# One transformer block on one core: x first in the queue, k/v weights in three pieces, identity products ahead of x

## The chip, the cores and the metric

The kernel runs on one core of one Trainium2 chip. The metric is the device time of one execution in microseconds. Of the kernel before, three runs are at hand: 1082.71, 1082.85 and 1082.98 us; the median is 1082.85.

## The reference

One encoder block, sequence 1024, width 1024, all in float32:

```
h = rmsnorm(x, norm1_g)
q, k, v, u = split(h @ w_in)              # widths 512, 128, 128, 512
a = attention(rope(rmsnorm(q)), rope(rmsnorm(k)), v)   # 8 query heads, 2 key/value heads of 64
p = (pool(u) - u) per group @ pool_w + pool_b, times pool_scale   # windows 2, 4, 8, 16
x = x + concat([a, p]) @ w_out
x = x + (silu(h2 @ w_gate) * (h2 @ w_up)) @ w_down     # h2 = rmsnorm(x, norm2_g), width 2816
```

## The kernel before

**Products.** Most operands of a product are split into two rounded parts, `hi` and `lo` (float32r), and a product is three TensorE passes over these parts (`PASSES`). Every split costs one copy (`hi`) and one subtraction (`lo`, line 355) on VectorE, ScalarE or GpSimd.

**The start.** x comes as eight tiles of 128 rows (`load_x`, line 434). TensorE turns each tile by eight transposes of 128x128 against the float32 identity (`turn_x`, line 474); ScalarE writes the `hi` part of each out of PSUM, scaled by a gain out of `pk` (line 464), and VectorE the `lo` part (line 466). `load_w` fetches weight blocks of `w_in` into one of three raw buffers (`NRAW`) and splits them into scratch tiles `wk`, of which there are 36 (`NSLOT`). The weights of k and v together are 256 columns wide and 8 blocks of 128 rows deep; before, they come as two pieces of four blocks, 512 KB each. `kv_tile(t)` (line 490) multiplies tile `t` of the turned x by them: per block k, three products of 256 columns.

**The order.** All is issued in the order written in the code. x's tiles are worked on in the groups [0], [1], [2, 3], [4, 5, 6, 7]. First the whole of group 0 is turned; then `weave` (line 933) alternates one k-step of k/v of a group with one transposed block of the next group. So the products of tile 0 are interleaved with the transposes of tile 1, and the transposes of tile 1 begin behind the first k-step of tile 0. TensorE carries this list out strictly in order. `stats_x` (line 447) adds the squares of a tile on ScalarE and takes the reciprocal root on VectorE by some twelve tiny operations (lines 362 to 373).

**The planner.** The order on VectorE, ScalarE and GpSimd, and which of them takes a split, come from `Flow`: it keeps a model of the time of each engine and of the DMA (`flow.load`), is run six times without a chip ahead of the build, and ranks jobs by the time at which TensorE needs them. In this model TensorE's steps cost double until 12 us (`COLD`). Both `load_x` and `load_w` tell it when data arrive.

**Queues.** All loads of the start go out on SyncE's queue in program order: `pk` (line 1523), x tile 0 in two halves, two weight pieces, x tiles 1 to 7, then the first u weights, gains, rope tables and the next u weights. A fetch into a raw buffer waits until the readers of that buffer's last content are done. `ident` is made by GpSimd at the very start, and `identr`, its rounded copy, by VectorE at line 384.

**PSUM.** `bank()` gives one of four banks of 512 columns, `bank2()` one of two double ones; `turn_x` uses both in turn.

Of the kernel before, what the change touches and what calls it, by code (L numbers as in the profile page):

```python
# [18 lines left out]
P = 128  # L19
# [3 lines left out]
NK = D // P  # L23
# [3 lines left out]
AW = NQ * HD  # L27
KW = NKV * HD
# [16 lines left out]
NRAW = 3  # L45
RIM, GAP = 120, 80
K = {
    "pieces": 2, "groups": [[0], [1], [2, 3], [4, 5, 6, 7]], "take": [0, 3], "tables": 2, "spread": [1],
    "ahead": [22, 39], "turn_k": 50, "wq": [60], "mix": [56, 62, 10, 30], "prep_q": [20], "turn_q": [37],
    "wo": [33, 39, 52, 62], "score": [40, 41, 42, 43, 47, 49, 52, 54, 57, 59, 61, 63, 63], "fold": 1,  # L50
    "out": [0, 0, 0, 2, 1, 2, 1, 2], "wo2": [3, 9, 10, 10, 16, 16], "mix_c": 5, "norm": 6, "next_prep": 8,
# [212 lines left out]
def act(n, extra=0.0):  # L264
    return "A", 0.1 + 0.00097 * n + extra


def dve(n):

    return "D", max(0.16, 0.07 + 0.00119 * n)  # L270
# [19 lines left out]
def block_kernel(  # L290
# [4 lines left out]
    nc = tc.nc  # L295
# [6 lines left out]
    w_in2, w_out2, w_gate2, w_up2, w_down2 = w_in[0], w_out[0], w_gate[0], w_up[0], w_down[0]  # L302
# [22 lines left out]
    flow = Flow(ranks)  # L325
    ffn = []

    def bank(dt=F32):
        flow.claim("b1", 4)
        return ps1.tile([P, 512], dt, tag="b1", name="b1")  # L330

    def bank2(dt=F32):
        flow.claim("b2", 2)
        return ps2.tile([P, 1024], dt, tag="b2", name="b2")

    def split(hi, lo, src, n, both=False):
        way = flow.quicker(act(n), dve_copy(n), pool_scale(n)) if both and not ffn else act(n)
        yield way
        if way[0] == "A":
            nc.scalar.activation(hi, src, AF.Copy)  # L340
        elif way[0] == "D":
            nc.vector.tensor_copy(hi, src)
        else:
            nc.gpsimd.tensor_scalar(hi, src, 1.0, 1.0, op0=ALU.mult, op1=ALU.mult)
        if both:
            yield from combine(n, lo, src, hi.bitcast(F32), ALU.subtract)
        else:
            yield dve(n)
            nc.vector.tensor_tensor(lo, src, hi.bitcast(F32), op=ALU.subtract)  # L349
# [33 lines left out]
    identr = held.tile([P, P], F32R, name="identr")  # L383
# [7 lines left out]
    def work(dt=F32, n=D):  # L391
        return wk.tile([P, n], dt, tag="wk", name="wk")
# [3 lines left out]
    def fetch(view, src, n=D):  # L396
        raw = rawp.tile([P, n], F32, tag="raw", name="raw")
        nc.sync.dma_start(view(raw), src)
        old = readers[-NRAW] if len(readers) >= NRAW else None
        readers.append(None)  # L400
        after = 0.0 if old is None else old.ready
        return raw, flow.load(P * n * 4, after), len(readers) - 1

    def consume(token, job):
        readers[token] = job
        return job
# [3 lines left out]
    def hT(a, k, c0, n):  # L410
        h, c = divmod(c0, HALF)
        o = (k % 2) * HALF + c
        return hs[a][h][k // 2][:, o:o + n]

    def load_w(col, n, per, apart=False):

        res = []
        for j in range(NK // per):
            raw, at, tok = fetch(
                lambda v: v.rearrange("p (k n) -> p k n", n=n),  # L420
                w_in2[j * per * P:(j + 1) * per * P, col:col + n].rearrange("(k p) n -> p k n", p=P))
            hi, lo = work(F32R), work(F32R)
            if not apart:
                job = consume(tok, flow.add(split(hi, lo, raw, D, both=True), at))
            for k in range(per):
                c = slice(k * n, (k + 1) * n)
                if apart:
                    job = consume(tok, flow.add(split(hi[:, c], lo[:, c], raw[:, c], n, both=True), at))
                res.append((hi[:, c], lo[:, c], job))
        return res  # L430
# [3 lines left out]
    def load_x(ts, pieces=1):  # L434
        n = D // pieces
        for t in ts:
            for i in range(pieces):
                nc.sync.dma_start(qp[:, t, i * n:(i + 1) * n], x2d[t * P:(t + 1) * P, i * n:(i + 1) * n])
                at = flow.load(P * n * 4)
                for k in range(i * n // P, (i + 1) * n // P):  # L440
                    x_at[t, k] = at
# [16 lines left out]
    def turn_x(ts):  # L458
        n = len(ts) * P
        c0 = ts[0] * P  # L460

        def evacuate(hi, lo, pt, k):
            yield act(n, 0.05)
            nc.scalar.activation(hi, pt[:, :n], AF.Copy, scale=g1[:, k:k + 1])
            yield dve(n)
            nc.vector.scalar_tensor_tensor(lo, pt[:, :n], g1[:, k:k + 1], hi.bitcast(F32), op0=ALU.mult, op1=ALU.subtract)

        for k in range(NK):
            flow.now = max([flow.now] + [x_at[t, k] for t in ts])
            wide = k % K["wide"] == K["wide"] - 1  # L470
            pt = bank2()[:, 0:512] if wide else bank()
            flow.tensor(0.107 * len(ts))
            for i, t in enumerate(ts):
                nc.tensor.transpose(pt[:, i * P:(i + 1) * P], qp[:, t, k * P:(k + 1) * P], ident)
            job = flow.add(evacuate(hT(0, k, c0, n), hT(1, k, c0, n), pt, k))
            flow.hold("b2" if wide else "b1", job)
            for t in ts:
                x_turned[t, k] = job
            yield

    E4 = HD // 4
    kv_job, kt_job, q_job = {}, {}, {}
# [410 lines left out]
    class OutProj:  # L893
# [5 lines left out]
        def run(self, n):  # L899

            for _ in range(min(n, NK - self.i)):
                k = KORDER[self.i]
                if self.i == 0:
                    self.py = bank()
                    if self.rows is None:
                        self.xr, at, self.tok = fetch(lambda v: v, x2d[self.t * P:(self.t + 1) * P, self.cs], 512)
                    else:
                        self.xr, self.tok = self.rows[0][:, self.cs], self.rows[2]
                j = attn_job[self.t]
                flow.tensor(0.681, wo[k][2], *(j[:1] if k >= 4 else j[1 + k // 2:2 + k // 2]))  # L910
                for i, (a, b) in enumerate(PASSES):
                    nc.tensor.matmul(self.py, mix[self.t][a][:, k, :], wo[k][b][:, self.cs], start=(self.i == 0 and i == 0), stop=(self.i == NK - 1 and i == 2))  # L912
                self.i += 1
                if self.i == NK:
                    job = flow.add(self.close())
                    flow.hold("b1", job)
                    x2_job[self.t, self.c] = consume(self.tok, flow.add(self.squares(job)))
# [15 lines left out]
    def weave(tiles, ts=None):  # L933
        turns = turn_x(ts) if ts else None
        for i, b in enumerate([b for g in [kv_tile(t) for t in tiles] for b in [g] * NK]):
            next(b, None)
            if turns and i % len(tiles) == 0:
                next(turns, None)
# [33 lines left out]
    def after(jobs):  # L972
        yield jobs
# [535 lines left out]
    def take_w(i):  # L1509
        g = order[i]  # L1510
        wus[g] = load_w(AW + 2 * KW + g * P, P, NK)

    def lean(phase):

        flow.load_of["D"] = K["load"][phase]
# [4 lines left out]
    ordered = tc.manual_schedule(engines=None)  # L1520
    ordered.__enter__()
    lean("x")
    nc.sync.dma_start(pk, packed)
    load_x([0], K["pieces"])
    wkv = load_w(AW, 2 * KW, 4, apart=True)
    load_x(range(1, NT))
    groups = K["groups"]
    run(turn_x(groups[0]))
    kf, tab_job = [], None
    for i, ts in enumerate(groups):  # L1530
# [17 lines left out]
    for i, g in enumerate(order):  # L1548
        for _ in pool_group(g):
            if at("spread", step):  # L1550
                spread_r(dgs, ones)
            for w in range(2):
                if K["ahead"][w] == step:
                    take_w(2 + w)
                if K["mix"][w] == step:
                    run(pool_mix(order[w]))
            if step == K["turn_k"]:
                flow.tensor(0, *kf)
                kt = k_turn()
            if step >= K["turn_k"]:  # L1560
                next(kt, None)
            if at("wq", step):
                wq = load_w(0, AW, 2)
            step += 1
# [148 lines left out]
```

## Time and profile before

| | us |
|---|---|
| median of three runs | 1082.85 |
| the profiled execution | 1083.04 |
| its span, first to last instruction | 1081.0 |
| TensorE busy (matmul) | 1061.1 |
| VectorE busy | 742.1 |
| ScalarE busy | 513.6 |
| GpSimd busy | 459.0 |

How to read it: PE is TensorE's matmul stream, PEld its weight loads, which run beside the matmuls; DVE is VectorE, ACT ScalarE, POOL GpSimd, SP SyncE. Times in a timeline count from the start of the span. A row of a timeline merges neighbours of one line; its second number runs from the start of the first to the modelled end of the last, so rows of TensorE overlap, and the pace of its steps is read from the starts. In brackets stands how long the engine was idle before, and what ended that. In the chain, each piece is the work that the next one waited for.

### The profile page before, as it was taken

How to read it: one execution, taken by the hardware profiler on the slowest of the kernel's cores; microseconds unless marked ns; L12 is line 12 of the kernel's file. 1: busy time of each engine (PE TensorE's matmuls, PEld its weight loads, DVE VectorE, ACT ScalarE, POOL GpSimd, SP SyncE). 2: the span in 40 equal slices, each digit the busy share in tenths (PEclk: the TensorE clock that was granted, in tenths of full speed). 3: DMA queues.
4: the chain of work that ended last, by engine and by line, in shares of the span. 5: the costliest groups of instructions: out<-in, count | busy, mean ns of one | idle time of the engine just before them, and what ended most of it. 6: DMA issues, size and time to landing. Idle time of an engine off the chain costs nothing.

```text
span 1081.0 us, 13923 instructions
## 1 busy us (share of the span) xinstructions
PE 1061.1 (98%) x5114; PEld 876.2 (81%) x5114; DVE 742.1 (69%) x1210; ACT 513.6 (48%) x912; POOL 459.0 (42%) x371
## 2 busy tenths in 40 slices
PE   7999999999999999999999999999999999999998
PEld 6887877878888888878878887888788878888787
DVE  7888678788776766784984479355954496448845
ACT  6614478666666654633343433434433443343340
POOL 3153444444223223463643555345534464445431
PEclk9999999999999999999999999999999999999999
DMA  7212110000000100221023102220212013110114
GB/s 260 69 40 79 39 59 30 10 21 10 20 21 11 30 21 30 59 98 39 19 68 109 39 1 78 78 79 1 78 59 76 23 33 104 59 40 20 40 58 156
DMA packets 42707, 58.47 MB, mean 54 GB/s; under 512 B 4240, under 2 KB 32784, under 8 KB 42640
## 3 DMA queue, kind: packets, MB, share of 16 engines
q1 hardware_dynamic: 42640, 57.59, 16.9%
q8 instruction: 40, 0.66, 0.2%
q14 instruction: 27, 0.22, 0.1%
HBM read 53.39 MB, written 4.19 MB: 53 GB/s over the span
## 4 chain that ended last, share of the span: by engine, by line
PE 79%; DVE 10%; issue 3%; POOL 3%; ACT 3%; DMA 1%; SPq 0%; POOLq 0%; ACTq 0%; DVEq 0%
PE b L1180 36%; PE b L912 8%; PE b L1498 8%; PE b L875 5%; PE b L832 5%; PE b L862 4%; PE b L688 4%; PE b L601 3%; DVE wk L355 3%; POOL wk L355 2%; PE b L1445 2%; DVE qp L1460 2%; PE b L490 2%; DVE ring L355 1%; DVE nm L841 1%
## 5 line engine op out<-in xcount | busy, mean ns | idle before, releaser
L1180 PE MATMUL b<-wk,ring 128*128 128x512 f32 x1872 | 426.8, 389 | 1.2 <-POOL ring L355 0.9
L1180 PEld LDWEIGHTS b<-wk,ring 128*128 128x128 f32 x1872 | 351.0, 188 | 75.6 <-POOL ring L355 1.8
L340 ACT ACTIVATE ring<-raw 128x512 fp32r<-128x512 f32 x130 | 81.5, 629 | 121.2 <-PE b L1180 59.9
L851 POOL TENSOR_SCALAR wk<-wk,rsm 128x1024 f32<-128x1024 f32 x64 | 75.0, 1180 | 132.9 <-PE b L862 40.7
L349 DVE TENSOR_TENSOR wk<-b,wk 128x512 fp32r<-128x512 f32 (+1 forms) x160 | 102.0, 659 | 42.5 <-ACT wk L340 42.1
L340 ACT ACTIVATE wk<-b 128x512 fp32r<-128x512 f32 (+1 forms) x160 | 90.4, 577 | 82.6 <-PE b L862 65.6
L355 POOL TENSOR_TENSOR ring<-raw,ring 128x512 fp32r<-128x512 f32 x49 | 63.3, 1292 | 149.5 <-ACT ring L340 136.0
L1498 PE MATMUL b<-raw,ring 128*128 128x512 f32 x480 | 113.4, 393 | 1.1 <-DVE qp L1460 1.1
L355 DVE TENSOR_TENSOR ring<-raw,ring 128x512 fp32r<-128x512 f32 x81 | 63.7, 789 | 72.2 <-ACT ring L340 71.7
L1498 PEld LDWEIGHTS b<-raw,ring 128*128 128x128 f32 x480 | 88.6, 188 | 24.3 <-DVE qp L1460 3.8
L1460 DVE TENSOR_TENSOR qp<-qp,b 128x512 f32<-128x512 f32 (+1 forms) x157 | 100.5, 673 | 9.0 <-PE b L1445 8.9
L912 PE MATMUL b<-wk 128*128 128x512 f32 x384 | 102.5, 397 | 0.0
L355 POOL TENSOR_TENSOR wk<-wk 128x512 fp32r<-128x512 f32 (+3 forms) x51 | 71.5, 1409 | 43.5 <-ACT wk L340 20.3
L832 PE MATMUL b<-kT,wk 128*128 128x512 f32 x256 | 89.4, 431 | 0.3 <-ACT wk L808 0.3
L875 PE MATMUL b<-wk,vv 128*128 128x512 f32 x256 | 82.7, 399 | 3.9 <-DVE wk L349 3.9
L841 DVE TENSOR_REDUCE nm<-b 128x1 f32<-128x1024 f32 x64 | 78.0, 1219 | 11.3 <-PE b L832 10.2
L1498 PE MATMUL b<-wk,ring 128*128 128x512 f32 x360 | 83.3, 389 | 0.0
L912 PEld LDWEIGHTS b<-wk 128*128 128x128 f32 x384 | 70.7, 188 | 14.9
L1498 PEld LDWEIGHTS b<-wk,ring 128*128 128x128 f32 x360 | 67.5, 188 | 14.2
L862 PEld LDWEIGHTS b<-ident,wk 128*128 128x128 f32 x512 | 63.6, 140 | 16.5
L862 PE MATMUL b<-ident,wk 128*128 128x128 f32 x512 | 76.4, 272 | 0.0
L843 ACT ACTIVATE wk<-b,nm 128x1024 f32<-128x1024 f32 x64 | 71.4, 1116 | 10.4 <-DVE nm L841 9.5
(144 smaller groups left out, 1445.1 us busy)
## 6 DMA issues: line engine op xcount, KB each, us to landing
raw<-in_w_gate_dram SPq DMA_DIRECT2D x22, 512.0 KB, 3.7
raw<-in_w_up_dram SPq DMA_DIRECT2D x22, 512.0 KB, 3.9
wk<-in_w_down_dram SPq DMA_DIRECT2D x20, 512.0 KB, 4.7
raw<-in_w_in_dram SPq DMA_DIRECT2D x10, 512.0 KB, 3.8
raw<-in_w_out_dram SPq DMA_DIRECT2D x8, 512.0 KB, 3.5
out_dram<-qp SPq DMA_DIRECT2D x15, 256.0 KB, 2.0
qp<-in_x_dram SPq DMA_DIRECT2D x7, 512.0 KB, 9.7
raw<-in_x_dram SPq DMA_DIRECT2D x14, 256.0 KB, 2.8
```

The source lines that it names most:

```text
L340: nc.scalar.activation(hi, src, AF.Copy)
L349: nc.vector.tensor_tensor(lo, src, hi.bitcast(F32), op=ALU.subtract)
L355: (nc.gpsimd if way[0] == "G" else nc.vector).tensor_tensor(dst, a, b, op=op)
L832: nc.tensor.matmul(s[:, c * 512:(c + 1) * 512], qT[t][0][:, h * P:(h + 1) * P], kT[:, kv, b, c * 512:(c + 1) * 512], start=(b == 0), stop= ...
L841: nc.vector.tensor_reduce(nm, s, axis=AX, op=ALU.max, negate=True)
L851: nc.gpsimd.tensor_scalar(pe, pe, rs, 1.0, op0=ALU.mult, op1=ALU.mult)
L862: nc.tensor.transpose(pt[:, j * P:(j + 1) * P], pe[:, c * P:(c + 1) * P], ident)
L875: nc.tensor.matmul(po[t, kv], vt, ps[:, b], start=(c == 0 and b == 0), stop=(c == NT - 1 and b == 1))
L912: nc.tensor.matmul(self.py, mix[self.t][a][:, k, :], wo[k][b][:, self.cs], start=(self.i == 0 and i == 0), stop=(self.i == NK - 1 and i == 2))
L1180: nc.tensor.matmul(bank_, w[0][:, a, i], x[:, b], start=(start and i == 0 and j == 0), stop=(stop and i == PARTS - 1 and j == 2), skip_gro ...
L1460: nc.vector.tensor_tensor(dst, dst, src, op=op)
L1498: nc.tensor.matmul(banks[t][0], x[:, a, t * P:(t + 1) * P], y[:, b], start=(own == name and i == 0 and j == 0), stop=(i == 1 and j == 2), ...
```

## The change

x tile 0 is loaded ahead of `pk`, in one piece of 512 KB. The weights of k and v come in three pieces of 2, 2 and 4 blocks (256, 256 and 512 KB), each in a raw buffer and a pair of scratch tiles of its own. Ahead of the first transpose, `keep_busy(24)` issues 24 TensorE products of the rounded identity with itself (128 columns each) into one PSUM bank that nobody reads. The existing `after([])` is an empty job that tells the planner that the bank is free. The planner's model isn't told of the 24 products.

```diff
@@ -45,7 +45,7 @@
 NRAW = 3
 RIM, GAP = 120, 80
 K = {
-    "pieces": 2, "groups": [[0], [1], [2, 3], [4, 5, 6, 7]], "take": [0, 3], "tables": 2, "spread": [1],
+    "busy": 24, "pieces": 1, "groups": [[0], [1], [2, 3], [4, 5, 6, 7]], "take": [0, 3], "tables": 2, "spread": [1],
     "ahead": [22, 39], "turn_k": 50, "wq": [60], "mix": [56, 62, 10, 30], "prep_q": [20], "turn_q": [37],
     "wo": [33, 39, 52, 62], "score": [40, 41, 42, 43, 47, 49, 52, 54, 57, 59, 61, 63, 63], "fold": 1,
     "out": [0, 0, 0, 2, 1, 2, 1, 2], "wo2": [3, 9, 10, 10, 16, 16], "mix_c": 5, "norm": 6, "next_prep": 8,
@@ -415,10 +415,12 @@
     def load_w(col, n, per, apart=False):
 
         res = []
-        for j in range(NK // per):
+        k0 = 0
+        for per in ([per] * (NK // per) if isinstance(per, int) else per):
             raw, at, tok = fetch(
-                lambda v: v.rearrange("p (k n) -> p k n", n=n),
-                w_in2[j * per * P:(j + 1) * per * P, col:col + n].rearrange("(k p) n -> p k n", p=P))
+                lambda v: v[:, 0:per * n].rearrange("p (k n) -> p k n", n=n),
+                w_in2[k0 * P:(k0 + per) * P, col:col + n].rearrange("(k p) n -> p k n", p=P), per * n)
+            k0 += per
             hi, lo = work(F32R), work(F32R)
             if not apart:
                 job = consume(tok, flow.add(split(hi, lo, raw, D, both=True), at))
@@ -477,6 +479,13 @@
             for t in ts:
                 x_turned[t, k] = job
             yield
+
+    def keep_busy(n):
+
+        pt = bank()
+        for _ in range(n):
+            nc.tensor.matmul(pt[:, 0:P], identr, identr, start=True, stop=True)
+        flow.hold("b1", flow.add(after([])))
 
     E4 = HD // 4
     kv_job, kt_job, q_job = {}, {}, {}
@@ -1520,11 +1529,12 @@
     ordered = tc.manual_schedule(engines=None)
     ordered.__enter__()
     lean("x")
+    load_x([0], K["pieces"])
     nc.sync.dma_start(pk, packed)
-    load_x([0], K["pieces"])
-    wkv = load_w(AW, 2 * KW, 4, apart=True)
+    wkv = load_w(AW, 2 * KW, (2, 2, 4), apart=True)
     load_x(range(1, NT))
     groups = K["groups"]
+    keep_busy(K["busy"])
     run(turn_x(groups[0]))
     kf, tab_job = [], None
     for i, ts in enumerate(groups):
```

## Rows read from the trace of the kernel before

**Rows 1.** The page: span; busy us, share of the span and instructions of each engine

```profile
span 1081.0 us, 13923 instructions
...
PE 1061.1 (98%) x5114; PEld 876.2 (81%) x5114; DVE 742.1 (69%) x1210; ACT 513.6 (48%) x912; POOL 459.0 (42%) x371
```

**Rows 2.** The chain of waits, 0 to 60 us: start us, us, what

```profile
3.13 7.49 DMA qp<-in_x_dram
...
12.63 0.21 PE b L474
12.85 0.64 PE b L490 x3
...
24.12 2.00 DVE wk L355
...
26.39 2.00 DVE ms L362
```

**Rows 3.** TensorE's timeline: start us, us, line, names, shapes, count [idle before, releaser]

```profile
4.35 1.30 PE L474 MATMUL b<-ident,qp 128*128 128x128 f32 x5 [4.35 <-DMA qp<-in_x_dram]
...
8.49 0.55 PE L490 MATMUL b<-wk 128*128 128x256 f32 x1 [1.69 <-DVE wk L342]
...
10.66 0.48 PE L474 MATMUL b<-ident,qp 128*128 128x128 f32 x1 [0.66 <-DMA qp<-in_x_dram]
...
15.79 0.27 PE L474 MATMUL b<-ident,qp 128*128 128x128 f32 x1
...
16.26 0.27 PE L474 MATMUL b<-ident,qp 128*128 128x128 f32 x1
```

**Rows 4.** Stretches: length, busy us of PE, PEld, DVE, ACT, POOL, clock, DMA, GB/s

```profile
6.74:8.05 1.31, 0.06 (x1) 0.00 (x0) 0.00 (x0) 1.31 (x4) 0.00 (x0) 1.00 0.99 339
...
10.66:15.79 5.13, 5.13 (x24) 5.13 (x25) 4.48 (x19) 2.19 (x6) 1.98 (x3) 1.00 1.03 420
...
8.05:17.00 8.95, 7.69 (x38) 7.13 (x39) 8.23 (x33) 3.39 (x10) 3.65 (x5) 1.00 1.03 406
17.00:31.80 14.80, 13.34 (x113) 12.78 (x113) 13.78 (x40) 11.57 (x26) 5.57 (x4) 1.00 0.57 157
```

**Rows 5.** SyncE's timeline, 0 to 40 us: the issues of DMAs

```profile
0.74 0.37 SPq L1523 DMA_DIRECT2D pk<-in_packed_dram  x1
1.16 0.90 SPq L438 DMA_DIRECT2D qp<-in_x_dram  x2
2.10 0.98 SPq L398 DMA_DIRECT2D raw<-in_w_in_dram  x2
...
9.39 0.38 SPq L398 DMA_DIRECT2D raw<-in_w_in_dram  x1
```

**Rows 6.** DMAs issued from 2.0 to 2.3 us: KB each, us to landing

```profile
raw<-in_w_in_dram SPq DMA_DIRECT2D x1, 512.0 KB, 5.9
```

**Rows 7.** Timeline of all engines, 0 to 45 us

```profile
1.33 0.23 DVE L384 CAST identr<-ident 128x128 fp32r<-128x128 f32 x1 [0.17 <-POOL ident masks.py:199]
...
4.83 2.46 ACT L464 ACTIVATE wk<-b,pk 128x128 fp32r<-128x128 f32 x8 [2.60 <-PE b L474]
5.23 1.51 DVE L466 SCALAR_TENSOR_TENSOR wk<-b,pk,wk 128x128 fp32r<-128x128 f32 x5 [3.40 <-ACT wk L464]
...
11.18 0.37 ACT L464 ACTIVATE wk<-b,pk 128x128 fp32r<-128x128 f32 x1 [2.85 <-PE b L474]
...
19.70 1.04 POOL L344 TENSOR_SCALAR wk<-raw 128x1024 fp32r<-128x1024 f32 x1 [4.48 <-DMA raw<-in_w_in_dram]
...
28.95 0.15 DVE L364 TENSOR_SCALAR ra<-ms 128x2 int32<-128x2 int32 x1
```

**Rows 8.** TensorE's timeline about single transposes of 128x128

```profile
4.35 0.45 PE L474 MATMUL b<-ident,qp 128*128 128x128 f32 x1 [4.35 <-DMA qp<-in_x_dram]
...
79.38 0.46 PE L578 MATMUL b<-identr,wk 128*128 128x128 f32 x4
79.68 0.47 PE L688 MATMUL b<-wk 128*128 128x512 f32 x1
```


## The prediction

> **What bounds the kernel now.** I read the page first: TensorE is busy 1061.1 of 1081.0 us [rows 1], so only some 20 us are not TensorE at work, and the change touches the start alone. The next view is the chain that ended last, in order of time: from 3.13 to 10.62 us it is one piece, the DMA of x, and behind that TensorE's own steps [rows 2]. TensorE's timeline shows the same as starts and waits: nothing before 4.35, transposes of x's first tile, the first k/v product at 8.49, and at 10.66 a stop for x's second tile (0.66 us) [rows 3]. That stop is a gate: the order of the code puts the first transpose of x's second tile behind the first k-step of k/v, so whatever is early before 10.62 waits there.
>
> Behind the gate a step is one transpose and three products of 256 columns. In the chain they advance by 0.21 + 0.64 = 0.85 us [rows 2]; from 15.79 to 16.26 the same step takes 0.47 [rows 3]. 0.64/3 = 0.213 us for 256 columns is 1.2 GHz at a column a cycle; the later pace is that of 2.4 GHz. The column of granted clock reads 1.00 in every stretch, 10.66 to 15.79 too [rows 4], so here the level has to be read from the pace of the steps: low up to about 15.8, high from there, after 5.1 us of TensorE without a pause.
>
> Last the stretches: TensorE fills 10.66 to 15.79 (5.13 of 5.13), but VectorE is close behind, 4.48 of 5.13 us; over 8.05 to 17.00 it is busy 8.23 of 8.95, over 17.00 to 31.80 13.78 of 14.80 [rows 4]. So TensorE at the low level bounds five microseconds, and VectorE is the next bound, less than a microsecond below. After that the kernel is TensorE's, and a shift at 31 us is kept to the end.
>
> **The change part by part.** The sum is made against the profiled execution: 1083.04 us, its span of 1081.0 and 2.04 around it, 0.19 above the median 1082.85 of the runs. The forecast is set down from the median.
>
> *x first in the queue, in one piece.* SP issues pk at 0.74 and x's halves from 1.16 to 2.06, then the weights [rows 5]. Now x's first tile goes out at 0.74, 0.42 earlier than its first half did, and pk behind it. The number of issues ahead of x's second tile stays five (pk, two halves, two weights; now x, pk, three weights), and so do the bytes. The stream is full from about 3 us on (0.99 of the 16 DMA engines just ahead of 8.05 [rows 4]), so all that follows moves with its start: by 0.42 at the best, by nothing if the early engines sit on issue latency. I take 0.4: the gate moves from 10.62 to 10.2. The first transpose loses nothing: it now waits for 512 KB instead of 256, 262 KB more at 339 GB/s [rows 4] being 0.77 us, less 0.42, so it could start at 4.7 instead of 4.35. pk, whose gains ScalarE needs for every evacuation, comes behind x by 44 KB, 0.13 us at that rate.
>
> *Weights of k and v in pieces of 2, 2 and 4 blocks.* The first piece took 5.9 us from its issue at 2.10, so it landed at 8.0, where VectorE's casts started [rows 5, 6]. Half the bytes are 0.77 us less, and 0.4 come from the stream: about 6.9. VectorE had been idle from 6.74 to 8.05 [rows 4], so 1.1 us of casts and subtractions come into a hole. The third piece takes the third raw buffer, so the next fetch (first u weights, issued at 9.39 [rows 5]) now waits for the readers of the first piece. On SP behind it stand gains, rope and the second u weights. The readers are two blocks' casts and subtractions, which begin at 6.9 instead of 8.0, and 9.39 covers them; the first use of these weights is at 19.70 [rows 7]. Cost: nothing, and at most some tenths that 10 us of cover hide. Two more scratch tiles of the 36 are held until k and v are done; later requests then fall sooner on slots of finished squares, which ScalarE alone wrote: nothing.
>
> *24 products of the identity.* They need the rounded identity, done at 1.56 [rows 7], and fill a TensorE that was idle until 4.35. The trace has no plain product of 128 columns. Lower end: four transposes of the same rounded type and shape take 79.38 to 79.68, 0.075 each, at the high level [rows 8]: 24 x 0.075 = 1.8 us. Upper end: a lone 128x128 transpose at the low level, 0.45 [rows 8]: 10.8 us. In between stand twice 0.075 (0.15, 3.6 us, end at 5.2) and the low pace of the unrounded transposes, 0.21 [rows 2] (5.0 us, end at 6.6). I take 0.15, the row of the same type at half the clock. x's first tile is then turned from 5.2 instead of 4.35. ScalarE's eight evacuations take 2.46 us at their own pace whatever TensorE's clock [rows 7], ending near 8.1; ScalarE then waited 2.85 us for the next transpose [rows 7], which hides that. VectorE's five halves behind them slip 0.85 too, and eat most of the hole that the early weights fill. Without that cover the price is the overshoot itself, 0.85 us. The one bank they write is overwritten later by the same engine: no wait.
>
> *The clock.* If TensorE is at the high level at the gate, the six steps that ran at 0.85 run at 0.47: 6 x 0.38 = 2.3 us off TensorE. Bounds: 0 and 2.3.
>
> The same is what the Trainium skill weighs in "TensorE: Matmul & The Clock Gate", section "Part 4: PE-mode transpose": a transpose does not count as a busy TensorE for the clock. The transposes from 4.35 to 6.8 here were followed by the low pace, which fits, though they were few. By it the 24 products alone have to raise the clock, and if they are too few, it is the second rival below.
>
> *The sum.* TensorE alone would give 0.4 + 2.3 = 2.7 us. VectorE does not: its work from 5.23 to 17.00 is 1.51 (the five halves [rows 7]) and 8.23, 9.7 us in 11.8. Started at 6.0 (after the overshoot) it ends at 15.7 without any idle time, and with 0.3 us of it at 16.0: 1.0 us sooner. Started at 5.2 it ends at 15.2: 1.8. TensorE's allowance lies above both, so VectorE decides; I take the middle, 1.4. From 17 to 31.8 the order and the clock stay, VectorE had 1.0 us idle there, and I give 0.1 of it. The rest is shifted. Total 1.5: 1082.85 - 1.5 = 1081.3 us, in a case of 1080.2 to 1082.2.
>
> What I can't work out is the planner: it orders VectorE, ScalarE and GpSimd by its own model, the new arrivals change that, and VectorE's chain has two pieces that are collisions: a 1024-column subtraction of 2.00 us and, at 26.39, two elements a partition that held 2.00 where the like takes 0.15 [rows 2, 7], each beside a GpSimd operation. One less or one more is 1.9 us either way; both ends stay in the range.
>
> **The rivals.**
> *TensorE sets the pace, VectorE follows.* The dummies end before x is there, the casts fit the hole, and the planner puts the root of the first tile's sums behind the halves, or loses one collision. For it: the six banks let TensorE run ahead of VectorE by some steps. Against: 0.65 us idle of 5.13 [rows 4]. Gain 2.7, with up to 1.9 for a collision: 1080.1, down to 1078.3.
>
> *The clock does not help.* It stays low under the dummies, or rises and falls again while TensorE waits for the gate (from about 7.5 to 10.2 it has three products to do). Then the steps run at 0.85 as before until near 15, and only the gate's 0.4 us stay: 1082.4 (1082.0 to 1082.9). For it: the transposes and scattered products from 4.35 to 10 did not raise it before. Against: with the dummies, TensorE has work from 1.6 on. The skill's rule on transposes speaks for this rival.
>
> *The dummies overshoot.* At 0.45 each they end at 1.56 + 10.8 = 12.4, past the gate; from 0.36 each ((10.2 - 1.56)/24) they are what TensorE waits for. x's first tile is turned from there; VectorE has by then the casts and subtractions behind it (4 of its 9.7 us), and needs 5.7 from 13.2 on: 18.9 instead of 17.0, +1.9, and with TensorE's steps and ScalarE's evacuations in that queue +2.5: 1084.8 to 1085.4. For it: no row shows such a product. Against: the rounded 256-column product costs 0.213, and half the columns should not cost more.
>
> **How the numbers follow.** Forecast 0.45, TensorE's pace 0.20, no help from the clock 0.25, overshoot 0.10. What this kernel's measurement can tell from no change is 0.2%, 2.2 us, so faster means under 1080.7 and slower over 1085.0. Faster: most of TensorE's pace (0.18) and 0.13 of the forecast, which a lost collision takes there: 0.31. Slower: most of the overshoot (0.07), and 0.03 for a collision more: 0.10. Same: 0.59. Range 1079.3 to 1083.5: it leaves out the overshoot and the deepest part of TensorE's pace.
>
> **What would show it.** TensorE's timeline: 24 products from 1.6, ending near 5.2 (overshoot: past 7); the gate near 10.2; steps of 0.47 right behind it (no help: 0.85). VectorE: casts from 6.9, and hardly any idle time from there to 16. VectorE's last of the evacuations that 17.00 to 31.80 holds starts near 30. The prediction is wrong if steps are fast behind the gate and the end moves by over 3 us or not at all: then VectorE was not the bound, or the planner's new order gives or takes more than the start.

## The result, and the profile after

The changed kernel takes 1088.59 us (median; 1088.43 to 1089.03) beside 1082.78 of the kernel before (1082.11 to 1082.98), a ratio of 1.0057 with a 95% interval of 1.0045 to 1.0069 (the ratios of this document are worked out from all runs and can differ in the last digits from the quotient of two medians). It is 5.8 us slower; forecast were 1081.3 us and a range up to 1083.5. The profiled execution took 1088.43, its span is 1086.6, 5.6 over that of [rows 1].

The page's first lines, after (busy us, share, instructions):

```profile
span 1086.6 us, 13965 instructions
...
PE 1068.2 (98%) x5138; PEld 880.0 (81%) x5138; DVE 733.8 (68%) x1211; ACT 513.1 (47%) x912; POOL 462.8 (43%) x370
```

The share of TensorE is 98% as in [rows 1], so this view can't tell where 5.6 us went. TensorE's timeline of the start (start us, us, line, names, count [idle before, releaser]), after:

```profile
1.62 5.39 PE L487 MATMUL b<-identr 128*128 128x128 f32 x24 [1.62 <-DVE identr L384]
6.80 1.29 PE L476 MATMUL b<-ident,qp 128*128 128x128 f32 x5
...
8.99 0.99 PE L499 MATMUL b<-wk 128*128 128x256 f32 x3
9.90 0.44 PE L476 MATMUL b<-ident,qp 128*128 128x128 f32 x1
...
12.51 0.31 PE L476 MATMUL b<-ident,qp 128*128 128x128 f32 x1
...
13.02 0.27 PE L476 MATMUL b<-ident,qp 128*128 128x128 f32 x1
...
14.69 0.35 PE L499 MATMUL b<-wk 128*128 128x256 f32 x1 [0.23 <-DVE rx L373]
15.40 0.50 PE L499 MATMUL b<-wk 128*128 128x256 f32 x2 [0.36 <-POOL wk L355]
```

and the stretches of [rows 4], after (length, busy us of PE, PEld, DVE, ACT, POOL, clock, DMA, GB/s):

```profile
8.05:17.00 8.95, 8.02 (x42) 6.66 (x42) 8.71 (x37) 6.72 (x19) 2.92 (x4) 1.00 1.04 407
17.00:31.80 14.80, 13.13 (x114) 12.92 (x114) 14.02 (x44) 10.68 (x23) 5.72 (x4) 1.00 0.53 142
```

Against [rows 3] the same work on TensorE is 2.45 us later at the first transpose (6.80 for 4.35), 0.76 earlier at the gate (9.90 for 10.66) and up to 1.7 earlier near 15.4. Then it gives this back: at 16.3 both kernels stand level, and the last group of transposes but two starts at 28.93 in place of 29.09, in both behind a wait for VectorE. Before, then after:

```profile
29.09 0.66 PE L474 MATMUL b<-ident,qp 128*128 128x128 f32 x4 [1.28 <-DVE wk L466]
```

```profile
28.93 0.66 PE L476 MATMUL b<-ident,qp 128*128 128x128 f32 x4 [1.67 <-DVE wk L468]
```

At 31 us 0.17 us are left, where 1.5 were forecast.

The loss comes 500 us later. Setting the same matmul of both traces side by side, after is still 0.2 us ahead at 480 us and 1.1 ahead at 489: before waits there twice for GpSimd's subtraction of `ring`, after once. TensorE's waits from 480 to 486.5 us (us in total, times, longest), before, then after:

```profile
PE b L1180 <- POOL ring L355: 0.9, 2, 0.6
```

```profile
PE b L1189 <- POOL ring L355: 0.7, 1, 0.7
```

From there it falls back by 1.35 us in each of five stretches: the sums down of the five feed-forward blocks (`down_sums`, L1498 before, L1507 after). From their first product to the first product behind them they last 38.89 to 38.97 us before and 40.24 to 40.30 after. After enters the first of them 1.1 us ahead (517.53 for 518.63), and 5 x 1.35 - 1.1 = 5.6 us, the whole loss. The same stretch on TensorE, with the first row behind it, before:

```profile
518.63 16.48 PE L1498 MATMUL b<-raw,ring 128*128 128x512 f32 x72
534.95 5.63 PE L1498 MATMUL b<-wk,ring 128*128 128x512 f32 x24
540.42 2.29 PE L1498 MATMUL b<-raw,ring 128*128 128x512 f32 x9
542.92 3.90 PE L1498 MATMUL b<-raw,ring 128*128 128x512 f32 x15 [0.22 <-DVE qp L1460]
546.66 11.04 PE L1498 MATMUL b<-wk,ring 128*128 128x512 f32 x48
557.54 4.70 PE L1180 MATMUL b<-wk,ring 128*128 128x512 f32 x20
```

and after:

```profile
517.53 16.48 PE L1507 MATMUL b<-raw,ring 128*128 128x512 f32 x72
533.85 6.00 PE L1507 MATMUL b<-wk,ring 128*128 128x512 f32 x24
539.70 2.63 PE L1507 MATMUL b<-raw,ring 128*128 128x512 f32 x9
542.57 1.20 PE L1507 MATMUL b<-raw,ring 128*128 128x512 f32 x4 [0.24 <-DVE qp L1469]
544.26 2.79 PE L1507 MATMUL b<-raw,ring 128*128 128x512 f32 x11 [0.50 <-DVE raw L355]
546.89 11.04 PE L1507 MATMUL b<-wk,ring 128*128 128x512 f32 x48
557.77 4.47 PE L1189 MATMUL b<-wk,ring 128*128 128x512 f32 x19
```

Read from start to start: the 72 products and the 48 take as long in both (16.32 and 10.88 us). The 24 between take 5.85 in place of 5.47, the nine 2.87 in place of 2.50, the fifteen 4.32 in place of 3.74: 0.38 + 0.37 + 0.58 = 1.33 us. The last piece has a releaser of its own, VectorE's `raw`. TensorE's waits, grouped (us in total, times, longest), after:

```profile
PE b L1507 <- DVE raw L355: 2.5, 5, 0.5
...
PE b L1507 <- DVE qp L1469: 1.2, 5, 0.2
```

Before has the second (1.1, 5, 0.2) and not the first. What VectorE does there, before:

```profile
542.97 1.00 DVE L355 TENSOR_TENSOR raw<-wk,raw 128x512 fp32r<-128x512 f32 x1
543.89 0.68 DVE L355 TENSOR_TENSOR ring<-silu,ring 128x512 fp32r<-128x512 f32 x1
```

and after:

```profile
542.43 1.17 DVE L355 TENSOR_TENSOR ring<-silu,ring 128x512 fp32r<-128x512 f32 x1
543.53 0.68 DVE L355 TENSOR_TENSOR raw<-wk,raw 128x512 fp32r<-128x512 f32 x1
```

The two subtractions have changed places. TensorE needs `raw` first, and it now ends at 544.21 in place of 543.97, for products that run 0.35 us earlier. No line of `down_sums` was edited: the order of these jobs is the planner's. It rehearses the kernel six times and keeps the rehearsal with the lowest time by its own model. With the old arrival times that was the second, with the new ones the fifth. By that model the kept rehearsal ends 0.6 us sooner than the one before (1085.26 for 1085.90); on the chip it is 5.8 us slower.

### The profile page after: what moved, and what is told of

The parts are those of the page before. It is cut to its first block, busy times and chain, and to the rows that moved or that the text cites. A ratio compares the mean times of both kernels' runs of the same rounds, so it can differ in the third digit from the quotient of the medians.

```text
span 1086.6 us, 13965 instructions
## 1 busy us (share of the span) xinstructions
PE 1068.2 (98%) x5138; PEld 880.0 (81%) x5138; DVE 733.8 (68%) x1211; ACT 513.1 (47%) x912; POOL 462.8 (43%) x370
## 4 chain that ended last, share of the span: by engine, by line
PE 78%; DVE 13%; issue 3%; POOL 3%; ACT 2%; DMA 0%; POOLq 0%; ACTq 0%
PE b L1189 36%; PE b L921 8%; PE b L1507 8%; PE b L884 5%; PE b L841 5%; PE b L871 4%; PE b L697 4%; PE b L610 3%; DVE wk L355 3%; DVE ring L355 2%; PE b L1454 2%; POOL wk L355 2%; DVE qp L1469 2%; PE b L499 1%; POOL ring L355 1%
## 5 line engine op out<-in xcount | busy, mean ns | idle before, releaser
L355 POOL TENSOR_TENSOR ring<-raw,ring 128x512 fp32r<-128x512 f32 x54 | 70.1, 1297 | 157.8 <-ACT ring L340 138.8
L1507 PE MATMUL b<-raw,ring 128*128 128x512 f32 x480 | 115.2, 394 | 4.1 <-DVE raw L355 2.5
L1507 PEld LDWEIGHTS b<-raw,ring 128*128 128x128 f32 x480 | 88.6, 188 | 29.1 <-DVE qp L1469 5.9
L355 DVE TENSOR_TENSOR ring<-raw,ring 128x512 fp32r<-128x512 f32 x76 | 57.8, 762 | 77.1 <-ACT ring L340 77.1
L355 POOL TENSOR_TENSOR wk<-wk 128x512 f32<-128x512 f32 (+3 forms) x50 | 73.7, 1481 | 34.6 <-ACT wk L340 16.5
L850 DVE TENSOR_REDUCE nm<-b 128x1 f32<-128x1024 f32 x64 | 78.0, 1219 | 11.2 <-PE b L841 10.2
L1507 PE MATMUL b<-wk,ring 128*128 128x512 f32 x360 | 85.1, 392 | 0.2
L355 POOL TENSOR_TENSOR ring<-silu,ring 128x512 fp32r<-128x512 f32 x35 | 54.0, 1542 | 63.3 <-ACT ring L340 63.3
L1507 PEld LDWEIGHTS b<-wk,ring 128*128 128x128 f32 x360 | 67.2, 188 | 16.5 <-DVE ring L355 1.8
```

The lines of the kernel that those rows point to most:

```text
L355: (nc.gpsimd if way[0] == "G" else nc.vector).tensor_tensor(dst, a, b, op=op)
L850: nc.vector.tensor_reduce(nm, s, axis=AX, op=ALU.max, negate=True)
L1507: nc.tensor.matmul(banks[t][0], x[:, a, t * P:(t + 1) * P], y[:, b], start=(own == name and i == 0 and j == 0), stop=(i == 1 and j == 2), ...
```

## The experiments

The theories. *Plan*: the new arrivals made the planner keep another order of work, and that order costs the five stretches. *Start*: the start itself (dummies, arrivals, clock) costs it. For the first two kernels of the table the order is taken from a planning with one kernel's start and replayed, job by job and engine by engine, on a program with the other's; the exchanged and the joined kernels replay an order that was edited in between. The core of that edit:

```
 def issue(self, limit):
+    if self.script:
+        return self.replay(limit)     # next (job, engine, step) of the script
...
-    best = min(best, (flow.now, ranks), key=lambda b: b[0])
+Flow.script = plan("before")          # or plan("after"); the start is built apart
```

All medians, with the kernel before run beside them; "stretch" is the length of the five `down_sums` stretches in the profile:

| kernel | start | order | median (range), us | before, us | ratio [95%] | stretch, us |
|---|---|---|---|---|---|---|
| new_start_old_plan | after | before | 1084.19 (1083.75–1085.91) | 1082.6 | 1.0017 [1.0008, 1.0026] | 38.93–38.94 |
| old_start_new_plan | before | after | 1089.15 (1088.86–1091.27) | 1082.6 | 1.0065 [1.0052, 1.0078] | 40.25–40.31 |
| new_busy0 | after, no dummies | its own | 1088.89 (1087.32–1090.08) | 1082.6 | 1.0057 [1.0045, 1.0070] | 40.25–40.31 |
| new_busy12 | after, 12 dummies | its own | 1088.51 (1087.48–1090.61) | 1082.6 | 1.0059 [1.0046, 1.0071] | 40.25–40.33 |
| old_exchanged | before | before, the pair exchanged | 1085.66 (1085.40–1085.94) | 1082.5 | 1.0028 [1.0017, 1.0040] | 39.53–39.55 |
| new_exchanged | after | after, the pair put back | 1085.79 (1085.50–1086.12) | 1082.5 | 1.0030 [1.0018, 1.0042] | 39.65–39.67 |
| new_start_joined | after | after, then before | 1081.82 (1081.64–1085.86) | 1082.5 | 0.9997 [0.9989, 1.0006] | 38.91–38.97 |
| new0_joined | after, no dummies | after, then before | 1081.00 (1080.55–1082.00) | 1082.5 | 0.9986 [0.9978, 0.9995] | 38.89–38.97 |
| dense_joined | after, products of ones | after, then before | 1081.76 (1081.43–1083.74) | 1082.42 | 0.9995 [0.9987, 1.0004] | 38.91–38.99 |
| old_fourth_plan | before | fourth rehearsal | 1092.07 (1089.82–1092.79) | 1082.42 | 1.0091 [1.0076, 1.0107] | 40.23–40.25 |
| only_x_first | x ahead of pk alone | its own | 1082.07 (1081.47–1082.35) | 1082.42 | 0.9997 [0.9988, 1.0006] | 38.90–39.00 |
| only_pieces | weights in pieces alone | its own | 1088.66 (1088.43–1089.35) | 1082.42 | 1.0059 [1.0046, 1.0072] | 40.24–40.29 |

**Start against order.**

> The changed start (x first, three weight pieces, 24 identity products), but VectorE, ScalarE and GpSimd carry out, job for job, the order and the engine choices that the planner made for the kernel before. Theory 'plan' (the 5.8 us are lost because the planner, run again on other arrival times, picked another order for the whole kernel): 1082.0 to 1083.2, and the five stretches of sums of the down projection, 1.35 us longer each in the changed kernel, are as long as before. Rival 'start' (the new start itself does it: raw buffers one turn further on, two more scratch slots held, TensorE 24 products longer): 1087.5 to 1089.

> The start of the kernel before, with the order and the engine choices that the planner made for the changed kernel. Theory 'plan': 1087.5 to 1089.5, with each of the five stretches of down sums 1.2 to 1.4 us longer than before. Rival 'start': 1082.5 to 1083.5.

The order carries the loss. On the untouched start the new order alone gives 1.0065, with all five stretches at 40.25 to 40.31 us; the changed start with the old order has them at 38.93. That run is still 1.6 us slower than before and lies above the 1082.0 to 1083.2 that *plan* had forecast for it. In its profile (1083.83 us, 0.8 over that of before) TensorE stands 0.4 us late from 16 us on, 1.7 at 27, 0.2 at 31 and 0.6 at the end; the rest of the 1.6 us lies in executions of which there is no trace.

**The dummies.** One line, `"busy": 24` to 0 and to 12:

> The changed kernel without the 24 identity products; the planner does not see them, so its order is that of the changed kernel. At 0.217 us each they ended at 6.8, 2.5 us after x was there. Theory 'the products cost a little more than they give' (their overshoot holds x's evacuations, the clock that they raise gives back 1.7 us of steps): 1087.5 to 1088.8. Rival 'they carry the start': without them the steps run at 0.85 until 15 and the end is 1.5 us later, 1089.8 to 1090.5. In both the five stretches of down sums stay as long as in the changed kernel.

> The changed kernel with 12 identity products instead of 24, ending near 4.2, when x's first tile lands at 4.3. If 12 raise the clock before the steps of the second tile: 0.7 to 1.5 us under the changed kernel, 1087.1 to 1087.9. If they are too few, the time is that of the kernel without them. Again the five stretches stay long.

Neither is told apart from the changed kernel, and new_busy0 lies between the ranges of its theory and its rival; the stretches are the same. The dummies did not cause the loss.

**The pair.** From the script, in each of the five blocks, one entry is moved past the other on VectorE:

```
+def exchanged(script, early, late):
+    log = list(script[0])
+    for k in range(5):
+        i, j = (next(p for p, r in enumerate(log) if r[0] == n + 144 * k and r[1] == "D") for n in (early, late))
+        n, e, _ = log.pop(i)
+        log.insert(j, (n, e, log[j - 1][2]))
...
+Flow.script = exchanged(plan("before"), 660, 665)   # old_exchanged
+Flow.script = exchanged(plan("after"), 665, 660)    # new_exchanged
```

> The kernel before, all its work in its own order, but in each of the five stretches of down sums VectorE carries out one pair the other way round, as in the changed kernel: the subtraction for a left operand (ring) first, the one for a right operand (raw) that TensorE needs sooner behind it. Theory 'the pair': TensorE waits 0.7 us more in each stretch, 5 x 0.73 = 3.6 us, 1085.8 to 1086.6. Rival 'the pair is hidden, the loss is the other switches of engine': 1082.3 to 1083.0.

> The changed kernel, with that one pair put back in each of the five stretches (right operand first). Theory 'the pair': 3.6 of the 6 us come back, 1084.6 to 1085.6; the other 0.63 us of each stretch stay. Rival: 1088 to 1089.

VectorE and TensorE in old_exchanged (L1560 is L1498, L408 is L355); the pair first:

```profile
542.56 1.18 DVE L408 TENSOR_TENSOR ring<-silu,ring 128x512 fp32r<-128x512 f32 x1
543.66 0.68 DVE L408 TENSOR_TENSOR raw<-wk,raw 128x512 fp32r<-128x512 f32 x1
```

```profile
542.69 1.20 PE L1560 MATMUL b<-raw,ring 128*128 128x512 f32 x4 [0.22 <-DVE qp L1522]
544.40 2.80 PE L1560 MATMUL b<-raw,ring 128*128 128x512 f32 x11 [0.50 <-DVE raw L408]
```

The exchange alone, in an otherwise untouched kernel, brings the wait of 0.50 us for `raw` and 0.62 us a stretch (39.54 for 38.92), 3.1 of the 3.16 us by which the kernel is slower. Put back in the changed kernel it takes the same 0.61 us a stretch out, and 0.73 stay. Expected were 0.73 a stretch; the two times lie 0.1 and 0.2 us outside the ranges given. Where the remaining 0.73 are is seen in new_exchanged (rows of all engines, one stretch):

```profile
534.20 6.04 PE L1560 MATMUL b<-wk,ring 128*128 128x512 f32 x24
...
535.06 0.81 DVE L408 TENSOR_TENSOR wk<-wk 128x512 f32<-128x512 f32 x1
535.28 1.74 POOL L408 TENSOR_TENSOR wk<-wk 128x512 fp32r<-128x512 f32 x1
...
536.03 1.55 DVE L408 TENSOR_TENSOR ring<-wk,ring 128x512 fp32r<-128x512 f32 x1 [0.15 <-ACT ring L393]
...
537.11 1.61 POOL L408 TENSOR_TENSOR raw<-wk,raw 128x512 fp32r<-128x512 f32 x1
537.50 1.77 DVE L408 TENSOR_TENSOR ring<-silu,ring 128x512 fp32r<-128x512 f32 x1
537.63 2.17 PEld L1560 LDWEIGHTS b<-wk,ring 128*128 128x128 f32 x10 [0.37 <-DVE ring L408]
...
541.72 0.53 PEld L1560 LDWEIGHTS b<-raw,ring 128*128 128x128 f32 x3 [0.51 <-DVE qp L1522]
```

and at the same place before:

```profile
536.03 1.30 POOL L355 TENSOR_TENSOR wk<-wk 128x512 fp32r<-128x512 f32 x1
...
536.77 1.11 DVE L355 TENSOR_TENSOR ring<-wk,ring 128x512 fp32r<-128x512 f32 x1 [0.28 <-ACT ring L340]
...
537.80 0.68 DVE L355 TENSOR_TENSOR wk<-wk 128x512 f32<-128x512 f32 x1
538.41 0.68 DVE L355 TENSOR_TENSOR ring<-silu,ring 128x512 fp32r<-128x512 f32 x1
```

TensorE's weight loads wait 0.37 us for a `ring` that VectorE gives out 3.38 us after the 24 products began (537.58 less 534.20); before it is 2.93 (537.88 less 534.95). VectorE's `wk<-wk` now runs ahead of that subtraction, beside GpSimd's, which takes 1.74 in place of 1.30, and the `ring` subtraction 1.55 in place of 1.11. The next subtraction, `ring<-silu`, grows most: 1.77 us in place of 0.68, beside GpSimd's `raw` (1.61 us from 537.11). The weight loads of the nine products then wait 0.51 us for VectorE's addition. So the place of the 0.73 us is shown; that the move of `wk<-wk` causes them is argued from these lines, and was not tried. The two plans differ in each block by more than that move (they also exchange some subtractions between VectorE and GpSimd), and none of this was tried alone.

**The joined order**: the order of after until the feed-forward blocks, that of before from there (`joined(plan("after"), plan("before"), 1350)`).

> The changed kernel with its own order up to the blocks of the feed-forward, and from there on job for job the order and engines of the kernel before. Theory 'the loss is all in the later order': the start's 0.2 us and 0.9 us of a vanished wait at 482 us remain, 1081.2 to 1082.2. Rival 'the start loses too, by its slower executions': 1083 to 1085.

> The same without the 24 identity products. Theory 'the products hold the start up': the second tile's gate is at 9.3 instead of 9.9 and x's evacuations 2.4 us earlier, 0.5 to 1.3 us under the kernel with them, 1080.2 to 1081.5. Rival 'the products are worth their time': the same or slower than with them.

With the old order in the blocks the changed kernel no longer loses anything; without its dummies it is 1.5 us faster than before (0.9986, interval below 1), the fastest kernel of all. Only part of that is the start's. In the profile of new_start_joined TensorE is 0.18 us ahead of before at 31 us and 1.0 at the end, in that of new0_joined 0.65 and 1.6; the other 0.9 us come between 480 and 490 us in both, from the new order there (old_start_new_plan gains them too, new_start_old_plan does not). Such leads compare single executions, and that of before (1083.04 us) is 0.5 over the median of its runs. Between these two kernels the dummies cost 0.8 us (1081.82 less 1081.00), but taking them out of the changed kernel gave nothing (new_busy0, 1088.89 for 1088.59), so their price is not settled. Nor did it come as expected: without them the gate was forecast for 9.3, and TensorE passed it at 10.06.

**Products of ones in place of the identity**, since a product that is mostly zeros might count for less:

```
+full = work(F32R, n=P)
+nc.vector.memset(full.bitcast(F32), 1.0)
-nc.tensor.matmul(pt[:, 0:P], identr, identr, start=True, stop=True)
+nc.tensor.matmul(pt[:, 0:P], full, full, start=True, stop=True)
```

> As new_start_joined, but the 24 products are of a block full of ones with itself instead of the identity, whose columns are nearly all zero (one VectorE memset more). In four runs with 24 identity products the clock rose between 10.9 and 16.2 us, without them between 12.2 and 15.9. Theory 'products of zeros do not count for the clock': it rises before the gate, by 9 us, and the second tile's steps all run at 0.47; 0.3 to 1.0 us under new_start_joined, 1080.8 to 1081.5. Rival 'the content does not matter': rise after 10.5, 1081.6 to 1082.3.

TensorE's timeline in it:

```profile
1.36 5.38 PE L542 MATMUL b<-wk 128*128 128x128 f32 x24 [1.36 <-DVE wk L540]
...
11.31 0.41 PE L529 MATMUL b<-ident,qp 128*128 128x128 f32 x1
12.01 0.27 PE L529 MATMUL b<-ident,qp 128*128 128x128 f32 x1
```

The 24 products take the same 5.38 us, and the low pace lasts until 11.8: the rival's forecast, and no sign that it matters what is multiplied.

**The planner alone, and the parts alone.** In the kernel before, the fourth rehearsal in place of the second, and nothing else (`best = (flow.now, ranks) if _ == 3 else best`); x ahead of `pk`; the pieces 2, 2, 4.

> The kernel before with nothing changed but the rehearsal whose ranks are taken: the fourth instead of the one that the planner picks. By the planner's own measure the two are equal within 0.1 us, but the fourth has the pair in the down sums the other way round. Theory 'a new plan costs as much without any new start': 1085.5 to 1089. Rival 'it took the new arrival times to spoil the order': 1082.3 to 1083.5.

> The kernel before with x's two halves ahead of pk in the queue, and nothing else; the planner does not see pk, so every engine's order is that of before. Theory 'the stream starts 0.4 us earlier and the gate moves with it': 1082.0 to 1082.5, second tile at 10.2 to 10.4. Rival 'TensorE and VectorE behind the gate take it back': 1082.5 to 1083.0.

> The kernel before with the weights of k and v in three pieces, and nothing else; the planner runs again on these arrival times. In its order the pair of the down sums is the other way round. Theory 'plan': 1085.5 to 1089.5, with the five stretches 0.6 to 1.4 us longer each. Rival 'it takes all parts together': 1082 to 1083.

Another rehearsal of the unchanged program costs 9.6 us in the median, more than forecast. The profiled execution was the fastest of the four (1089.82, 6.8 over that of before), with 6.6 us in the five stretches (5 x 1.32); what the slower ones lose beyond that no trace shows. x first alone changes nothing that can be measured in the median, and the plan stays the same (the planner's model knows nothing of `pk`); its profile, of the fastest of 11 executions (1081.47), is 1.6 us below that of before. The pieces alone move the planner, to the sixth rehearsal, and give the whole loss, 1.0059, again with the five stretches at 40.24 to 40.29 us. So of the edits it is the pieces that cost, and not by their transfers: in the profile of only_pieces TensorE is 2.3 us ahead of before at 31 us and 5.2 behind at the end. x in one piece was not tried alone.

## Why the prediction was wrong

The step that failed is the planner's: "One less or one more is 1.9 us either way; both ends stay in the range." The term was taken as 0, within 1.9 either way, and measured 6.6 us (old_start_new_plan, 1089.15, less 1082.6 before). It was bounded by two collisions on VectorE in the first 31 us, as if a new order could only differ where the arrivals differ. But the planner picks a whole rehearsal, for all 1081 us, and the choice turned over. The prediction names this among its signs of being wrong ("the planner's new order gives or takes more than the start"), but gave it no price beyond the two collisions. Within the first 31 us the bound did hold: of its two collisions one went from 2.00 to 1.22 us, and in place of the other VectorE's next tiny operation took 1.63.

With it falls "After that the kernel is TensorE's, and a shift at 31 us is kept to the end." The small shift of 0.17 us was kept to 480 us. Where the plan stays, a larger one is kept too (only_x_first: 1.66 us at 31, 1.68 at the end); where the plan turns over it is not (only_pieces: 2.3 us at 31, 0.6 at 480). That TensorE is 98% busy doesn't make the rest of the kernel independent of the other engines' order: the products of `down_sums` take their operands from VectorE with nothing to spare. Before, `raw` is done at 543.97, and the weight load that needs it has already waited for it:

```profile
544.02 2.38 PEld L1498 LDWEIGHTS b<-raw,ring 128*128 128x128 f32 x11 [0.34 <-DVE raw L355]
```

Two exchanged subtractions of 0.7 to 1.2 us turn that into a wait of TensorE, five times.

The start's own steps, term by term:

- *x first*: its first tile was forecast for 4.7 and landed at 4.31; the gate for 10.2 and landed at 9.77 (TensorE 9.90). Right in mechanism, 0.4 too cautious. Over all profiles the second tile lands at 9.1 to 9.9 with x first and at 10.6 to 11.0 without.
- *Pieces*: the first was forecast for 6.9; VectorE's first cast starts at 5.42:

```profile
0.74 0.37 SPq L440 DMA_DIRECT2D qp<-in_x_dram  x1
...
5.42 0.29 DVE L342 CAST wk<-raw 128x256 fp32r<-128x256 f32 x1 [3.58 <-DMA raw<-in_w_in_dram]
...
7.94 1.13 DVE L468 SCALAR_TENSOR_TENSOR wk<-b,pk,wk 128x128 fp32r<-128x128 f32 x4 [2.22 <-ACT wk L466]
```

That gain did not last: by 7.94 VectorE stands idle again for 2.22 us, because the sums of x's first tile (VectorE's `lo` parts, the subtractions out of PSUM) begin there and not at 5.23 [rows 7]. The next weight fetch, which the prediction saw covered at 9.39, goes out at 10.10; no wait that this caused was found.
- *24 products*: 0.15 us each were chosen; they took (6.80 - 1.62) / 24 = 0.216. The prediction named the nearer row, the low pace of 0.21 [rows 2], and took the other. They end 2.5 us after x's landing and hold the first transpose 2.45 us back, not 0.85. That is the overshoot rival in small: at most 0.8 us (new0_joined), not the 3.5 to 4 that it had at 0.45 each over the forecast.
- *The clock*: the rival that it doesn't help was nearer. The steps behind the gate run at 0.85 us until 12.51 and at 0.46 from 13.02; the dummies had not raised it by the gate.
- *VectorE decides*: right, and more than forecast: TensorE's longest wait between 9 and 31 us is that of 1.67 for VectorE's sums. It is busy 8.71 of 8.95 us up to 17.00, and over both stretches 22.73 us in place of 22.01 [rows 4]: the sums of 128 columns are sixteen there (4.9 us) in place of eleven (3.7), since those of x's first tile, held back by the products of the identity, now lie behind 8.05. So of 1.5 us 0.17 are left at 31.

So the sign of the forecast holds for the start, but hardly its size: 0.17 us in the trace at 31 us. In the median the kernel with the blocks' old order is 0.7 us faster than before, which its interval doesn't tell from no change, and most of that comes from the order near 482 us.

## What to carry to other kernels

Where a program orders the work from a model of times, an edit of the arrival times is an edit of the whole order: compare the order of every engine in both kernels, far behind the edit as well, before putting a price on the edit itself, and pin the order when only the edit is to be measured. Two plans that the planner rates alike within 0.1 us were 9.6 us apart on the chip in the median, so the last choice between its rehearsals is better made by timing them. A bound engine at 98% says that there is little idle time, not that its suppliers have slack: look at how late each operand is ready.

## What was not expected of the hardware

- A product of 128 rounded columns takes 0.216 us at the low level, as long as one of 256 columns (0.213 [rows 2]); identity or ones make no difference (5.39 and 5.38 us for 24). That this is the low level is read from the work behind them, whose steps still take 0.85 us.
- 5.2 us of products without a pause, from 1.62 to 6.80, were not followed by the high level of 2.4 GHz. The fast steps began between 10.9 and 16.2 us in the five profiles with 24 dummies (12.6 in the changed kernel), at 15.9 with 12, and between 12.2 and 15.9 in the eight without. The mean granted clock of the whole span reads 1.00 in all of them, and in the stretches of the start too ([rows 4] and those after), so the pace of the steps has to be read. The Trainium skill, "TensorE: Matmul & The Clock Gate", Part 1, says that the array starts at half rate until activity releases it, and that the number of slow products varies between runs of one kernel; the slow steps at the start agree with the first; for the second no kernel here has two traces, though the spread over kernels would fit it. Dummies ahead of the data were no sure way to the high level here.
- The same kernel can spread by more than such a start is worth: new_busy0 ran from 1087.32 to 1090.08 us in five executions, so a gain of half a microsecond is not told from the spread. That the moment at which the clock rises makes this spread is not shown.
